# A hybrid layer's first block makes its output product by seven block products, and the sums are made elsewhere

## The chip, the cores and the metric

The kernel runs on one core of one Trainium2 chip. The time is that of the device, in microseconds (us): the median of the runs shown is compared. The engines are named as in the profile: PE (TensorE's matmuls) with PEld (its weight loads), DVE (VectorE), ACT (ScalarE), POOL (GpSimd) and SP (SyncE, which here only issues DMAs). POOL issues DMAs too.

## The reference

One layer is computed for a prompt of 2048 tokens and a sample of 64, each token a vector of 1024 numbers in 32-bit floats. All matrices below are 1024 x 1024 except the gate and projection of `p`.

```
h = rms_norm(x, g_pre)
vA, bA, cA, zA, q, f, iv, zB, gA, gB = split(h @ w_in)        # ten products
yA = (silu(zA) * bA * causal_conv3(cA * vA)) @ w_a_out        # path A
o  = hgrn2_scan(silu(q), 1 - fg, iv, log(fg)), normed         # path B, fg from f
yB = (o * silu(zB)) @ w_b_out
merged = sigmoid(gA) * yA + sigmoid(gB) * yB
out = merged @ w_o
x = x + rms_norm(out, g_post)                                 # first norm
gate = sigmoid(rms_norm(x, g_ple) @ w_ple_gate)               # second norm
x = x + (p @ w_ple_proj) * gate
```

## The kernel before

**Blocks.** The 2112 tokens are handled in three blocks of 768, 704 and 640 (`SIZES`, line 35). Everything lies with features on the 128 partitions and tokens along the row, so a 1024 x n activation is eight tiles of 128 x n. Each block has two token halves of 384, 352 or 320; that is the width of its matmuls.

**Matmuls in three parts.** A number is split into a high half, which the 32-bit matmul format takes as it is, and a low half, the rest (`split`, line 220: ACT casts, DVE subtracts). A product is hi x hi + hi x lo + lo x hi: three matmuls, which is why they come on lines 412 to 414, 559 to 561 and 594 to 596 in threes. The weights are split too. A low half that is used again is stored in DRAM ("low") and loaded later on SP's queue (line 269) instead of being computed again; `used_later` (line 245) decides which are stored.

**Seven products.** Most weight products are made by the seven products of Strassen's method in Winograd's form: a pair of column tiles and the two halves of the depth make a 2 x 2 matrix of blocks A11, A12, A21, A22, the activations likewise B11 to B22, and with sums S1 to S4 of the A's and T1 to T4 of the B's seven products replace eight. One product here is 4 k x 3 = 12 matmuls. `sgroup` (line 397) makes all seven for one pair of tiles, one after another; it makes the gates and most of `w_in`. `in_turn` (line 527) makes the first of the seven for all four pairs, then the second for all four, and so on; its operands (`operand_of`) are split just ahead of their product. In the middle and the last block W_A (`w_a_out`), W_B (`w_b_out`) and W_O (`w_o`) go this way. In the first block they go by plain products: `gemms` (line 637) and `gemm` load 8 x 2 weight tiles of 128 x 512 and make 384 matmuls for each matrix.

**The sums of the weights.** S1 to S4 and their low halves have to be in DRAM before `in_turn` can use them. `prepare_sums` (line 359) makes them in four groups for each matrix. A group loads four weight tiles, forms four sums on DVE (lines 387 to 393), stores each (line 376), splits it and stores its low half (line 379); all its DMAs are on POOL's queue. In the first block it makes those of W_A and W_B, in steps put into the loops of `merge`, with three buffers named "s" for the low halves (`shared`); low halves that `in_turn` and `sgroup` load use the same three buffers for three of every seven (`low_tile`). In the middle block it makes those of W_O in path A, with ring tiles instead.

**The end of a block.** `merge` (or `merge_in_turn`) makes yA, yB and the merged tiles; then W_O (`final_out`, or `out_in_turn`); then, while PE works on the next block's first seven gate groups (`run(fills, LEAD)`, 7 x 7 = 49 products), the steps of `final_norm` (line 1281) are put between the products; then `final_gate`. `operands` (line 755) makes the next block's T1 to T4 during W_O. The norm's steps: squares of W_O's result (`sum_squares`, ACT squares and DVE adds on line 707), column sums over the partitions by PE (`col_rstd`, line 685) and a power on POOL, a spread of the factors by PE (line 669), eight tiles scaled and added to x with their squares summed, the column sums and spread of the second norm, eight tiles split for `final_gate`.

**What sets the order.** A scheduler orders each engine's instructions by program order, marked priorities and its own estimate of times, and the order is then fixed. Weight loads and casts are marked urgent. `spread_out` (line 1349) puts a plan into `hooks`: one entry after each product, a number that says how many steps of the norm run there. `placed()` keeps a step's matmuls from going ahead of the product that they are put behind, and `behind_all` does that on the other engines. The plan for the norm was, in the middle block,

```
(1, 1, 1, 1, 0, 1, 0, 1) + (0, 1) * 8 + (0, 0, 1, 0, 1) + (0, 1) * 8
```

that is: four steps of squares, column sums at hook 5, spread at 7, eight norm steps, the second norm's column sums at hook 26 and spread at 28, eight splits up to hook 44. In the first block it was `(0, 1, 0, 1) + (0, 1, 0) * 8 + (0, 0, 1, 0, 1) + (0, 1) * 8`, with the squares made during W_O.

Of the kernel before, what the change touches and what calls it, by code (L numbers as in the profile page):

```python
# [93 lines left out]
def hybrid_step(  # L94
# [31 lines left out]
    def nm(s):  # L126
        uid[0] += 1
        return f"{s}_{uid[0]}"
# [113 lines left out]
    def sum_tile(dt=F32):  # L242
        return wp.tile([P, 4, P], dt, tag="s", name=nm("s"), bufs=3)

    def used_later(idx, part):

        if GA * 8 <= idx < GB * 8 + KB - 2:
            return part in ("S1", "S2", "S3", "S4")  # L250
        if idx in (GB * 8 + KB - 1, QQ * 8):
            return part != 0
        if W_A <= idx < W_G:
            lower = (idx - W_A) % KB >= KH
            return not lower if idx >= W_O and part == 0 else lower if idx < W_O and part == 1 else idx >= W_O
        return True

    def split_w(raw, key=None, spread=False):
# [100 lines left out]
    def prepare_sums(firsts, shared):  # L359


        groups = [(idx + g, idx + KH + g) for idx in firsts for g in range(KH)]

        def tile_of(dt=F32):
            return rt(4 * P, dt).rearrange("p (k c) -> p k c", c=P)

        def load(i1, i2):
            out = [tile_of() for _ in range(4)]
            for t, (i, h) in zip(out, ((i1, 0), (i2, 0), (i2, 1), (i1, 1))):
                G.dma_start(t, w_blk[i, h])  # L370
            return out

        def keep(name, i1, s):
            sums.setdefault(i1, {})[name] = dram.tile([P, 4, P], F32, tag=f"{name}_{i1}", name=nm(name), bufs=1)
            lows[i1, name] = dram.tile([P, 4, P], F32, tag=f"lo{name}_{i1}", name=nm("low"), bufs=1)
            G.dma_start(sums[i1][name], s)
            lo = sum_tile(F32R) if shared else tile_of(F32R)
            split(s, lo, lo)
            G.dma_start(lows[i1, name], lo.bitcast(F32))

        nxt = load(*groups[0])
        yield
        for n, (i1, _) in enumerate(groups):
            a11, a21, a22, a12 = nxt
            if n + 1 < len(groups):
                nxt = load(*groups[n + 1])
            V.tensor_tensor(a22, a21, a22, ALU.add)
            keep("S1", i1, a22)
            V.tensor_tensor(a21, a11, a21, ALU.subtract)
            keep("S3", i1, a21)  # L390
            V.tensor_tensor(a11, a22, a11, ALU.subtract)
            keep("S2", i1, a11)
            V.tensor_tensor(a12, a12, a11, ALU.subtract)
            keep("S4", i1, a12)
            yield
# [238 lines left out]
                hook()  # L634
        return pss

    def gemms(idx0, act, segs, by_k=False, late=KB - 1):

        j0, j1 = 0, KB
        if len(segs) > 1:  # L640
            yield from gemm_late([idx0, idx0 + 1], act, segs, late)
            j0 = 2
        if by_k:
            j1 -= 2
        for j in range(j0, j1):
            yield gemm(idx0 + j, act, segs)
        if by_k:
            yield from gemm_by_k([idx0 + j for j in range(j1, KB)], act, segs)


    def tiles_of(n):
# [103 lines left out]
    def operands(hc, rs, load, early=False):  # L755


        pair = None
        for i in range(KH):
            pair = pair or [load(k) for k in (i, i + KH)]  # L760
            for k, xk in zip((i, i + KH), pair):
                scaled_x(xk, k, rs)
            hc["B11"].append(narrow(half(pair[0], 0)))
            yield
            sums_of(hc, pair)
            yield
            hi, lo = split_rt(pair[1])
            hc["B21"].append((half(hi, 0), half(lo, 0)))
            hc["B22"].append((half(hi, 1), half(lo, 1)))
            pair = [load(k) for k in (i + 1, i + 1 + KH)] if early and i + 1 < KH else None  # L770
            yield

    ends, summed = [], []
# [404 lines left out]
            paced(dma)  # L1178
        return t

    def merge(bl, a, kept, extra):

        segs = bl["segs"]
        ob, m, mg, loaded = [], [], [], {}

        def fetch(kind, j):
            if j < KB:
                loaded[kind, j] = reload(kept[kind, j])

        fetch(GA, 0)  # L1190
        fetch("o", 0)
        for j, pss in enumerate(gemms(W_A, a, segs)):
            fetch(GA, j + 1)
            fetch("o", j + 1)
            if j == KB - 1:
                fetch(GB, 0)
            sg = loaded.pop((GA, j))
            for s, ps in zip(segs, pss):
                V.tensor_tensor(sg[:, cols_of(s)], ps, sg[:, cols_of(s)], ALU.mult)
            m.append(sg)  # L1200
            ob.append(split_rt(loaded.pop(("o", j))))
            if j in (2, 4, 6):
                next(extra, None)
        for j, pss in enumerate(gemms(W_B, ob, segs)):
            fetch(GB, j + 1)
            sg = loaded.pop((GB, j))
            for s, ps in zip(segs, pss):
                V.tensor_tensor(sg[:, cols_of(s)], ps, sg[:, cols_of(s)], ALU.mult)
            V.tensor_tensor(sg, sg, m[j], ALU.add)  # L1209
            mg.append(split_rt(sg))  # L1210
            if j in (0, 2, 4, 6, 7):
                next(extra, None)
        return mg

    def merge_in_turn(a, kept, mg):

# [28 lines left out]
            dict(idx=W_B, order=IN_TURN, raw=ob, sink=sink_b, anew=("A11", "A12")),  # L1245
        ], loads

    def final_out(segs, mg, xo, acc):

        for j, pss in enumerate(gemms(W_O, mg, segs, True)):  # L1250
            xo.append(rt())
            for s, ps in zip(segs, pss):
                A.copy(xo[j][:, cols_of(s)], ps)
            if j < KB - 2:
                sum_squares(j, xo[j], acc, width[0])
            yield
        for j in range(KB - 2, KB):
            sum_squares(j, xo[j], acc, width[0])
        yield

    def out_in_turn(mg, xo, acc, last):


# [14 lines left out]
        stage["sink"] = sink  # L1278
        return stage

    def final_norm(bl, segs, xo, acc, h2, kept, squares=False):


        c = slice(segs[0]["off"], segs[-1]["off"] + hn())
# [189 lines left out]
    for bi, bl in enumerate(blocks):  # L1474
# [26 lines left out]
        if first:  # L1501
            next(sums_ahead)
        mg, xo, h2, acc = [], [], [], rt()
        if first:
            mg = merge(bl, a, kept, sums_ahead)
        else:
            stages, loads = merge_in_turn(a, kept, mg)
            stages.append(out_in_turn(mg, xo, acc, bl["last"]))
            loads(W_A, -1)
            for idx, n in in_turn(stages, a_first):  # L1510
                loads(idx, n)
                if nxt and (idx, n) == (W_B, 6):
                    hc = new_operands()
                    with sized_to(nxt):
                        ops = sized(nxt, operands(hc, spread_all(cols), partial(load_x, nxt), True))
                    spread_out((ops, (0, 1, 0, 1, 0, 1, 0) * KH))
                elif nxt:
                    pass
                elif (idx, n) == (W_B, 5):
                    ph = [split_rt(raw) for raw in load_p(bl, G)]  # L1520
                elif (idx, n) == (W_O, 4):
                    norms = [final_norm(bl, [s], xo, acc, h2, None) for s in segs]
                    spread_out((norms[0], (1, 0, 1, 1, 1, 0, 1, 0)))
            if nxt:
                xo.extend(stages[-1]["mid"])
        if nxt:
            if first:
                hc = new_operands()
                with sized_to(nxt):
# [67 lines left out]
```

## Time and profile before

| | |
|---|---|
| median of 3 runs | 2611.29 us (2609.13 to 2613.52) |
| profiled execution | 2615.63 us, span 2613.6 us |
| granted PE clock, mean | 0.998 |
| PE, DVE, ACT, POOL busy | 99%, 65%, 56%, 14% |
| DMA | 717.92 MB, mean 275 GB/s |
| first block: W_A, W_B, W_O | from 700.7, about 768 and 836.8 us |
| next block's leading gate groups | 904.1 to about 1008 us |
| middle block: W_A, W_B, W_O, gate groups | from about 1590, 1644, 1698 and 1755 us |

A row of a group reads: line, engine, operation, output <- input with shape, count, busy us and mean ns of one. A row of waits reads: who waited for whom, us in total, times, longest. A row of the timeline has start and duration in us, and in brackets the time that its engine was idle before it and what ended that. PEq, SPq and POOLq are the engines' queues. Times of instructions overlap in PE's pipeline, so the pace is read from their starts. The tile names of this program: `pg` and `pa` are PSUM tiles, `raw`, `hi` and `lo` weights and their halves, `s` the three shared buffers, `S` and `low` the sums and low halves in DRAM, `r` the 48 ring tiles, `hf` half tiles.

### The profile page before, as it was taken

What the parts mean: (1) busy time and instruction counts of PE and PEld (TensorE: products, weight loads), DVE (VectorE), ACT (ScalarE), POOL (GpSimd) and SP (SyncE); (2) the same over time, 40 slices, a digit from 0 to 9 for tenths busy, and PEclk for the clock granted to TensorE, in tenths of its full rate; (3) what the DMA queues carried; (4) which work ended last, traced back from release to release, by engine and by line L of the source; (5) the groups of instructions that cost most, each with busy time, mean ns of one, the idle gap of its engine ahead of it and who ended that gap; (6) DMA issues with size and microseconds to landing.
All of it is one profiled execution on the core that took longest, in us unless ns stands there. A gap on an engine that the chain in (4) does not pass through costs nothing. (4 is left out here: it accounts for less than half of the span.)

```text
span 2613.6 us, 47303 instructions
## 1 busy us (share of the span) xinstructions
PE 2588.3 (99%) x16532; PEld 2575.7 (99%) x16532; DVE 1710.0 (65%) x3417; ACT 1472.4 (56%) x2852; POOL 352.9 (14%) x653
## 2 busy tenths in 40 slices
PE   8999999999999999999999999999999999999999
PEld 8999999999999999999999999999999999999998
DVE  7887788788757665465564456887435555336867
ACT  6655565554433564466564555566456665446675
POOL 2000000110143121111111221102100001001111
PEclk9999999999999999999999999999999999999999
DMA  8677667788788598866768998988887877999985
GB/s 322 219 243 243 230 224 245 268 300 269 266 330 281 197 324 266 284 222 205 266 225 284 354 383 310 323 276 310 294 278 246 268 249 261 299 299 312 339 269 202
DMA packets 350686, 717.92 MB, mean 275 GB/s; under 512 B 42960, under 2 KB 47600, under 8 KB 350448
## 3 DMA queue, kind: packets, MB, share of 16 engines
q1 hardware_dynamic: 312624, 566.17, 64.3%
q0 software_dynamic: 37536, 148.68, 15.7%
q8 instruction: 130, 2.13, 0.3%
q14 instruction: 108, 0.88, 0.1%
q10 hardware_dynamic: 288, 0.05, 0.0%
HBM read 521.52 MB, written 193.22 MB: 273 GB/s over the span
## 5 line engine op out<-in xcount | busy, mean ns | idle before, releaser
L412 PE MATMUL pg<-r,hi 128*128 128x320 f32 (+2 forms) x3304 | 1084.7, 328 | 0.7 <-ACT hi L220 0.7
L413 PE MATMUL pg<-r,hi 128*128 128x320 f32 (+2 forms) x3304 | 1068.4, 323 | 0.0
L414 PE MATMUL pg<-r,lo 128*128 128x384 f32 (+2 forms) x2356 | 768.3, 326 | 4.2 <-DMA lo<-low 4.2
L268 ACT CAST hi<-raw 128x512 fp32r<-128x512 f32 x678 | 417.7, 620 | 485.5 <-PE pg L413 176.2
L412 PEld LDWEIGHTS pg<-r,hi 128*128 128x128 f32 x3304 | 622.1, 188 | 1.6 <-ACT hi L220 1.0
L413 PEld LDWEIGHTS pg<-r,hi 128*128 128x128 f32 x3304 | 622.4, 188 | 0.0
L414 PEld LDWEIGHTS pg<-r,lo 128*128 128x128 f32 x2356 | 442.7, 188 | 5.6 <-DMA lo<-low 5.6
L414 PE MATMUL pg<-r,s 128*128 128x352 f32 (+1 forms) x948 | 300.5, 317 | 1.7 <-DMA s<-low 1.7
L220 ACT CAST hi<-raw 128x512 fp32r<-128x512 f32 x276 | 168.8, 621 | 199.9 <-PE pg L595 66.0
L595 PE MATMUL pg<-r,hi 128*128 128x384 f32 (+2 forms) x768 | 253.4, 330 | 0.0
L594 PE MATMUL pg<-r,hi 128*128 128x384 f32 (+2 forms) x768 | 253.0, 330 | 0.2 <-ACT hi L268 0.2
L220 DVE TENSOR_TENSOR lo<-raw,hi 128x512 fp32r<-128x512 f32 x248 | 169.6, 688 | 102.7 <-ACT hi L220 99.8
L596 PE MATMUL pg<-r,lo 128*128 128x384 f32 (+2 forms) x688 | 228.1, 332 | 0.0
L560 PE MATMUL pg<-r,hi 128*128 128x352 f32 (+1 forms) x656 | 207.0, 317 | 0.0
L559 PE MATMUL pg<-r,hi 128*128 128x352 f32 (+1 forms) x656 | 204.5, 318 | 0.0
L220 DVE TENSOR_TENSOR r<-r,r 128x320 fp32r<-128x320 f32 (+7 forms) x282 | 172.9, 632 | 43.9 <-ACT r L220 43.1
L220 ACT CAST hi<-s 128x512 fp32r<-128x512 f32 x160 | 99.2, 620 | 173.0 <-PE pg L413 161.5
L414 PEld LDWEIGHTS pg<-r,s 128*128 128x128 f32 x948 | 178.8, 189 | 2.5 <-DMA s<-low 2.5
L220 ACT CAST r<-r 128x320 fp32r<-128x320 f32 (+7 forms) x282 | 153.1, 574 | 40.8 <-DVE r L1209 11.9
L426 ACT COPY hf<-pg 128x352 f32<-128x352 f32 (+2 forms) x354 | 156.7, 445 | 5.4 <-PE pg L414 5.2
L220 DVE TENSOR_TENSOR lo<-s,hi 128x512 fp32r<-128x512 f32 x160 | 110.3, 690 | 63.5 <-ACT hi L220 58.7
L594 PEld LDWEIGHTS pg<-r,hi 128*128 128x128 f32 x768 | 144.0, 188 | 0.4 <-ACT hi L268 0.4
(394 smaller groups left out, 4113.3 us busy)
## 6 DMA issues: line engine op xcount, KB each, us to landing
raw<-w_blk SPq DMA_DIRECT2D x586, 256.0 KB, 3.9
raw<-S SPq DMA_DIRECT2D x408, 256.0 KB, 4.1
lo<-low SPq DMA_DIRECT2D x398, 256.0 KB, 3.9
low<-lo SPq DMA_DIRECT2D x287, 256.0 KB, 3.2
s<-low SPq DMA_DIRECT2D x280, 256.0 KB, 3.9
S<-s SPq DMA_DIRECT2D x152, 256.0 KB, 2.9
r<-w_blk POOLq DMA_DIRECT2D x48, 256.0 KB, 6.7
S<-r POOLq DMA_DIRECT2D x48, 256.0 KB, 6.3
```

The costliest lines, as they stand in the source:

```text
L220: return A.copy(hi, src).ins, V.tensor_tensor(lo, src, hi.bitcast(F32), ALU.subtract).ins
L268: A.copy(hi, raw)
L412: add(hi[:, k, :], xhi, start=start and k == 0, stop=False)
L413: add(hi[:, k, :], xlo, start=False, stop=False)
L414: last[0] = add(lo[:, k, :], xhi, start=False, stop=k == KH - 1).ins
L426: copied = A.copy(got[n], ps[bank])
L559: add(hi[:, k, :], xhi, start=start and k == 0, stop=False)
L560: add(hi[:, k, :], xlo, start=False, stop=False)
L594: T.matmul(ps, hi[:, k % 4, :], xhi[:, c], start=k == ks[0], stop=False)
L595: T.matmul(ps, hi[:, k % 4, :], xlo[:, c], start=False, stop=False)
L596: last[0] = T.matmul(ps, lo[:, k % 4, :], xhi[:, c], start=False, stop=k == ks[-1]).ins
```

## The change

The first block's W_O goes through `in_turn` with `out_in_turn`, like the middle block's; `final_out` goes away and `gemms` loses its options. `merge` becomes a generator, leaves the merged tiles unsplit, and makes the first operands of W_O after its seventh W_B tile; at that point the next block's first x tiles and spread factors are asked for as well (`next_ops`). `prepare_sums` makes W_O's and W_A's sums in the first block and W_B's in the middle block. For W_O it also makes and stores the low halves of A11, A12 and A22 (`keep_low`), which the plain products stored before. `final_norm` makes the squares itself in the first block too, both blocks use one plan, and in it the second norm's column sums stand at hook 28 and the last split at hook 46.

```diff
@@ used_later
-        if W_A <= idx < W_G:
-            lower = (idx - W_A) % KB >= KH
-            return not lower if idx >= W_O and part == 0 else lower if idx < W_O and part == 1 else idx >= W_O
+        if W_A <= idx < W_O:
+            return part == 1 and (idx - W_A) % KB >= KH
@@ prepare_sums
+        def keep_low(key, s):
+            lows[key] = dram.tile([P, 4, P], F32, tag=f"lo{key}", name=nm("low"), bufs=1)
+            lo = sum_tile(F32R) if shared else tile_of(F32R)
+            split(s, lo, lo)
+            G.dma_start(lows[key], lo.bitcast(F32))
...
-        for n, (i1, _) in enumerate(groups):
+        for n, (i1, i2) in enumerate(groups):
             a11, a21, a22, a12 = nxt
             if n + 1 < len(groups):
                 nxt = load(*groups[n + 1])
+            if i1 >= W_O:
+                for key, s in (((i1, 0), a11), ((i1, 1), a12), ((i2, 1), a22)):
+                    keep_low(key, s)
@@ operands
+        pair = [load(k) for k in (0, KH)]
+        yield
         for i in range(KH):
-            pair = pair or [load(k) for k in (i, i + KH)]
...
-            pair = [load(k) for k in (i + 1, i + 1 + KH)] if early and i + 1 < KH else None
+            pair = [load(k) for k in (i + 1, i + 1 + KH)] if i + 1 < KH else None
@@ merge
-            mg.append(split_rt(sg))
+            mg.append(sg)
             if j in (0, 2, 4, 6, 7):
                 next(extra, None)
-        return mg
+            yield
@@ final_norm
-        if squares:
+        if kept is not None:
             for j in range(KB):
                 sum_squares(j, xo[j], acc, width[0])
@@ the loop over blocks
-        sums_ahead = prepare_sums((W_A, W_B), True) if first else prepare_sums((W_O,), False) if bi == 1 else iter(())
+        sums_ahead = prepare_sums((W_O, W_A), True) if first else prepare_sums((W_B,), False) if bi == 1 else iter(())
...
+        def next_ops():
+            with sized_to(nxt):
+                made = sized(nxt, operands(hc, spread_all(cols), partial(load_x, nxt)))
+                next(made)
+            return made
...
+        stages = [out_in_turn(mg, xo, acc, bl["last"])]
         if first:
-            mg = merge(bl, a, kept, sums_ahead)
+            for j, _ in enumerate(merge(bl, a, kept, mg, sums_ahead)):
+                if j == KB - 2:
+                    a_first.extend(narrow(half(t, 0)) for t in mg[:KH])
+                    ops = next_ops()
+            spread_out((ops, (0, 1, 0, 1, 0, 1, 0) * KH))
+            loads = lambda idx, n: None
...
-            if first:
-                hc = new_operands()
-                with sized_to(nxt):
-                    ops = sized(nxt, operands(hc, spread_all(cols), partial(load_x, nxt)))
-                for j, _ in enumerate(final_out(segs, mg, xo, acc)):
-                    if j in (1, 3, 5, 7):
-                        run(ops, 3)
-            norm = sized(bl, final_norm(bl, segs, xo, acc, h2, kept, not first))
-            start = (0, 1, 0, 1) + (0, 1, 0) * KB if first else (1, 1, 1, 1, 0, 1, 0, 1) + (0, 1) * KB
-            spread_out((norm, start + (0, 0, 1, 0, 1) + (0, 1) * KB))
+            norm = sized(bl, final_norm(bl, segs, xo, acc, h2, kept))
+            spread_out((norm, (1, 1, 1, 1, 0, 1, 0, 1) + (0, 1) * KB + (0, 0, 0, 0, 1, 0, 1) + (0, 1) * KB))
```

More of the change, by code (lines that the diff above doesn't have):

```diff
@@ L635, in gemm_by_k, with gemms @@
         return pss
[L637 to L645, printed above, removed]
+    def gemms(idx0, act, segs):
+        yield from gemm_late([idx0, idx0 + 1], act, segs, KB - 1)
+        for j in range(2, KB):
             yield gemm(idx0 + j, act, segs)
-        if by_k:
-            yield from gemm_by_k([idx0 + j for j in range(j1, KB)], act, segs)
     def tiles_of(n):
@@ L1246, in merge_in_turn @@
         ], loads
[L1248 to L1259, printed above, removed]
     def out_in_turn(mg, xo, acc, last):
@@ L1509, in hybrid_step @@
+        if first:
+            for j, _ in enumerate(merge(bl, a, kept, mg, sums_ahead)):
[4 more added lines that the diff above has]
+            loads = lambda idx, n: None
+        else:
+            before, loads = merge_in_turn(a, kept, mg)
+            stages = before + stages
             loads(W_A, -1)
-            for idx, n in in_turn(stages, a_first):
-                loads(idx, n)
-                if nxt and (idx, n) == (W_B, 6):
-                    hc = new_operands()
-                    with sized_to(nxt):
[L1515 to L1523, printed above, removed]
```

34 lines of the change are left out of this document (19 added, 15 removed).

## The prediction

> **What bounds the kernel now.** I read the page's busy times first, then what PE waited for, then windows over the stages that the change touches.
>
> ```profile
> PE 2588.3 (99%) x16532; PEld 2575.7 (99%) x16532; DVE 1710.0 (65%) x3417; ACT 1472.4 (56%) x2852; POOL 352.9 (14%) x653
> ```
>
> ```profile
> PE pa L1153 <- ACT r L220: 6.9, 1, 6.9
> PE pg L414 <- DMA lo<-low: 4.2, 5, 1.6
> PE pa L685 <- DVE r L707: 3.3, 2, 2.7
> ```
>
> PE is busy for 99% of the span. Its largest wait (6.9 us) is at the very start, where the change does not reach. So the time moves only if PE gets less to do, gets new gaps, or loses old ones; work on other engines counts only where it makes a gap. In the windows, the columns are length, then busy us and instructions of PE, PEld, DVE, ACT, POOL, then granted clock, DMA share and GB/s. The rows are the first block's W_A, its W_O, its seven leading gate groups, and the middle block's W_O.
>
> ```profile
> 700.70:768.00 67.30, 67.30 (x385) 67.30 (x384) 48.72 (x76) 26.59 (x42) 31.80 (x60) 1.00 0.91 339
> ```
>
> ```profile
> 836.80:904.10 67.30, 67.30 (x387) 67.30 (x386) 44.29 (x65) 31.36 (x55) 9.69 (x18) 1.00 0.65 215
> 904.10:998.00 93.90, 91.04 (x575) 89.91 (x575) 63.28 (x95) 59.37 (x108) 17.54 (x30) 1.00 0.85 297
> ```
>
> ```profile
> 1698.00:1752.00 54.00, 53.52 (x327) 51.77 (x326) 47.00 (x94) 38.18 (x82) 4.28 (x8) 1.00 0.86 287
> ```
>
> The first block's W_O has PE full at clock 1.00 with DMA only 65% busy. The middle block already does its W_O by seven products, so its row shows what the first block will look like.
>
> **Part 1: PE's work in the first block's W_O.** Its edges on PE's timeline:
>
> ```profile
> 836.79 0.42 PE L594 MATMUL pg<-r,hi 128*128 128x384 f32 x1
> ```
>
> ```profile
> 903.92 0.34 PE L596 MATMUL pg<-r,lo 128*128 128x384 f32 x1
> 904.10 0.32 PE L412 MATMUL pg<-r,hi 128*128 128x352 f32 x1
> ```
>
> By the code that is 8 column tiles x 2 token halves x 8 k x 3 = 384 matmuls from 836.79 to 904.10: 67.31 us, 0.1753 us each (durations overlap, so the step counts and not the 0.34). Seven products are 7 x 4 x 4 x 3 = 336, of the same width. 48 go: 48 x 0.1753 = **-8.4 us**, all on the path, since PE never paused here.
>
> **Part 2: what feeds those products.** Out go 16 weight loads, 16 casts, 16 subtractions, 12 stores of low halves on SP's queue, and the eight splits of the merged tiles. In come, on SP's queue, 28 loads of weights or sums and 28 of low halves, 56 x 256 KB = 14.7 MB in 58.9 us, 249 GB/s; 28 casts; 28 operand splits with their sums. The middle block does the same instruction list on 352 columns: DVE 47.0 of 54 us, DMA 0.86. Scaled by 384/352, DVE needs at most 51 of 58.9 us. PE paid this there:
>
> ```profile
> 1727.54 0.75 PE L559 MATMUL pa<-r,hi 128*128 128x352 f32 x3 [0.22 <-ACT r L220]
> 1728.45 0.43 PE L560 MATMUL pa<-r,hi 128*128 128x352 f32 x1 [0.16 <-DVE r L220]
> ```
>
> I take the same 0.38: **+0.4**. Where the two blocks differ is DMA that is left over at the start. The sums come in eight groups on POOL's queue, paced by the merge loop, and the last begins inside W_O:
>
> ```profile
> 841.85 0.69 DVE L387 TENSOR_TENSOR r<-r,r 128x512 f32<-128x512 f32 x1 [4.08 <-DMA r<-w_blk]
> ```
>
> ```profile
> r<-w_blk POOLq DMA_DIRECT2D x48, 256.0 KB, 6.7
> S<-r POOLq DMA_DIRECT2D x48, 256.0 KB, 6.3
> low<-s POOLq DMA_DIRECT2D x32, 256.0 KB, 5.6
> ```
>
> ```profile
> r<-x_fm POOLq DMA_DIRECT2D x16, 352.0 KB, 7.0
> ```
>
> A group is 4 loads, 4 sums, 4 low halves: 3.1 MB. It now meets a stage that itself asks for 249 GB/s, plus the next block's x. Bounds: 0, if the prefetched weights cover it, to 3 us (3.1 MB over about 14 us is 220 GB/s; with 249 and x some 500 against the 406 quoted below, so a quarter of 14 us). I take 1, nearer zero, since by the code four casts and seven low halves can lie ready: **+1.0**.
>
> **Part 3: sums and low halves.** W_O's four groups each write three more low halves: 12 casts, 12 subtractions and 12 issues on POOL, beside W_A and the start of W_B.
>
> ```profile
> L220 ACT CAST hi<-s 128x512 fp32r<-128x512 f32 x160 | 99.2, 620 | 173.0 <-PE pg L413 161.5
> ```
>
> ```profile
> L220 DVE TENSOR_TENSOR lo<-s,hi 128x512 fp32r<-128x512 f32 x160 | 110.3, 690 | 63.5 <-ACT hi L220 58.7
> ```
>
> ```profile
> ACT s L220 <- DMA low<-s: 16.9, 11, 4.0
> ```
>
> 12 x 0.62 = 7.4 us of ACT and 12 x 0.69 = 8.3 of DVE, in a window where DVE is busy 48.7 and ACT 26.6 of 67.3 us, and the merged tiles' splits leave the same loop: hidden, 0. The wait that is added: ACT waits for one of three "s" buffers until a low half is stored (so far 16.9 us over 32 of them, 4.0 at most). Queued behind it are the weight casts, and on POOL the fetches of the saved gates. At the same rate 12 more cost ACT 6 us of waiting, spread over four groups; PE showed no gap in W_A with the earlier 16.9. I take 0, with those 6 us as the upper end.
>
> W_B's sums move to the middle block's path A, where W_O's were, by the same instructions. They are wanted one stage (54 us) earlier; the last low half is issued there at 1565 (the row), and W_B begins near 1644:
>
> ```profile
> L379 POOL DMA_DIRECT2D low<-r x16: 542/542/547, 1481.3 to 1565.4; - x16
> ```
>
> Hidden, 0. So is the next block's first x pair, asked for two products earlier.
>
> **Part 4: the second norm, middle block.** Its column sums stand on PE's queue (L685), and PE stopped there for the last squares:
>
> ```profile
> 1811.19 0.89 DVE L707 TENSOR_TENSOR r<-r,r 128x704 f32<-128x704 f32 x1
> ```
>
> ```profile
> 1812.23 2.45 PE L685 MATMUL pa<-ones,r 128*128 128x1 f32 x12 [2.73 <-DVE r L707]
> ```
>
> ```profile
> 1814.96 0.47 PE L414 MATMUL pg<-r,lo 128*128 128x320 f32 x1
> 1815.23 0.47 PE L412 MATMUL pg<-r,hi 128*128 128x320 f32 x1
> ```
>
> ```profile
> 1820.91 0.31 PE L414 MATMUL pg<-r,lo 128*128 128x320 f32 x1
> 1821.06 0.31 PE L412 MATMUL pg<-r,hi 128*128 128x320 f32 x1
> ```
>
> ```profile
> 1809.40:1812.20 2.80, 0.10 (x1) 0.00 (x0) 2.74 (x6) 1.63 (x3) 0.54 (x1) 1.00 0.99 338
> 1812.20:1814.70 2.50, 2.47 (x13) 2.50 (x14) 0.85 (x3) 0.00 (x0) 0.88 (x1) 0.56 1.02 405
> 1814.70:1819.40 4.70, 4.70 (x19) 4.70 (x20) 0.65 (x2) 1.78 (x4) 1.99 (x3) 0.51 0.81 293
> ```
>
> The gap is 2.73 us, and behind it the granted clock is 0.56 and then 0.51 until 1819.4. There a matmul steps 0.27 instead of 0.15: 17 of them cost 2.0 more, and the 12 column sums 1.06 more than the undisturbed 1.39 below. The stall is worth 2.73 + 2.0 + 1.06 = 5.8 us. How far does it move? The plan lets the sums go after 27 products (hook 26); by the count below they stood after 111/4 = 27.75. After the change they may go after 29.
>
> ```profile
> 970.54 1.39 PE L685 MATMUL pa<-ones,r 128*128 128x1 f32 x12
> ```
>
> ```profile
> 1755.20:1809.40 54.20, 34.14 (x111) 20.73 (x111) 1.00 0.86 299
> ```
>
> So 1.25 products move ahead, 15 matmuls x 0.1465 = 2.2 us; 0.5 of the gap stays, too short to lower the clock (1.59 below did not). Gain 2.2 + 3.06 = **-5.2**. Bounds: 0, if the squares come as much later, to -5.8.
>
> **Part 5: the first block's gates.** Its final norm takes the middle block's rhythm: the eight squares leave W_O for four steps here, the eight norm steps come every second product instead of every third, and the second norm after 29 products instead of 31. Gaps, first and middle block:
>
> ```profile
> 911.59 0.43 PE L412 MATMUL pg<-r,hi 128*128 128x352 f32 x1 [0.75 <-ACT hi L220]
> 939.89 0.43 PE L414 MATMUL pg<-r,s 128*128 128x352 f32 x1 [0.52 <-DMA s<-low]
> 949.49 0.43 PE L414 MATMUL pg<-r,lo 128*128 128x352 f32 x1 [1.59 <-DMA lo<-low]
> ```
>
> ```profile
> 1757.96 0.41 PE L414 MATMUL pg<-r,s 128*128 128x320 f32 x1 [0.95 <-DMA s<-low]
> 1796.17 0.41 PE L414 MATMUL pg<-r,lo 128*128 128x320 f32 x1 [1.02 <-DMA lo<-low]
> ```
>
> ```profile
> 936.00:950.00 14.00, 11.89 (x72) 11.31 (x72) 9.20 (x14) 6.81 (x13) 2.15 (x4) 1.00 1.03 406
> ```
>
> The first block pays 2.9 us now, the middle one 2.0 besides its norm. In the new rhythm DMA is asked for more (x in and out within 3.9 instead of 5.8 us), against a ceiling seen at 406 GB/s. I take 2.0 + the 0.5 of part 4, less 2.9, so about 0, **+0**; bounds -2.9 (all gaps gone) and +5.8 (the whole norm stall appears here). The middle block's last splits come two products later too, at the 47th of 49; 3.5 us remain for a cast and a subtraction: 0.
>
> **Sum:** -8.4 + 0.4 + 1.0 - 5.2 + 0 = -12.2 us. The profiled execution took 2615.63 us (span 2613.6 and 2.0 around it), 4.3 above the median of 2611.29 and above the slowest shown, 2613.52. I take the same difference off both: 2603.4 profiled and **2599.1** in the median.
>
> **A rule weighed.** The row says that 2.73 us of idling halved the clock. [...]
>
> **The rivals.**
> A. The clock fell in the profiled execution only, or the norm's sums are as late as before: of 5.2 us only 2.2, or nothing, is there in the median. For it: the profile is 4.3 us slower than the median. Against: the order is fixed in the program. Time 2611.3 - 8.4 + 1.4 - 2.2 = 2602.1, or 2604.3 with no gain at all.
> B. The first block gets the norm stall that the middle one had, 5.8 us, with 3 us of waits at the start of W_O: 2599.1 + 5.8 + 2.0 = 2607. For it: the same rhythm, DMA at its ceiling. Against: 29 products instead of 27, and each product is 10% longer there.
> C. Slower: W_A's sums slide into W_O. Three "s" buffers serve both the sums' low halves and three of seven of the products' low loads; the latter have priority. W_O's 58.9 us carry 58.9 x 406 = 23.9 MB; its weights and x take 14.7 + 2.9, so it decides from two groups (6.3 MB) on. All four are 12.6 MB, 30.2 in all, 74 us instead of 59: +15 us, and where the waits come as five gaps like the 2.73, each costs 3.06 more: 2614 to 2629. Against: the groups are tied to the merge loop, and now only the last one begins 5 us into W_O.
> D. The waits for low halves in the gates (2.9 + 2.0) go as well: 2594.
>
> **How the numbers follow.** The forecast has 0.50, A 0.15, B 0.15, C 0.10, D 0.10. 0.2%, about what can be told from no change, is 5.2 us here: faster is below 2606.1, slower above 2616.5. The forecast, A, D and a little of B are faster: 0.77; the rest of B and the low end of C are the same: 0.14; C's upper part is slower: 0.09. The range goes from D's 2594 less a microsecond to past B: 2593 to 2611; the forecast alone has 2595 to 2604.
>
> **What would show it.** Right: 16484 matmuls on PE; L594 to L596 without the first block's W_O, and 128x384 matmuls on lines 559 to 561 for some 59 us; no gap at L685 in the middle block and no clock of 0.5 there. Wrong: a clock below 1.00 after the first block's W_O begins; waits for lo<-low or s<-low of more than 3 us within it; sums (L387) still being made well after its start; L685 waiting for L707 in the first block.

## The result, and the profile after

The change makes the kernel faster by a quarter of a percent: median 2604.98 us (2603.03 to 2611.69, 11 runs) against 2611.29 us (2607.77 to 2615.26, 11 runs); ratio 0.9976, 95% interval 0.9968 to 0.9984, so 4.2 to 8.4 us less. The forecast was 2599.1, 12.2 us less: the sign is right, and nearly half of the gain is missing. The profiled execution of the changed kernel took 2604.98 us, its span 2603.2.

The page of the changed kernel, busy times:

```profile
PE 2579.6 (99%) x16484; PEld 2566.8 (99%) x16484; DVE 1729.1 (66%) x3469; ACT 1487.7 (57%) x2896; POOL 358.5 (14%) x665
```

The 48 matmuls are gone. PE was busy 8.7 us less. What PE waited for in the changed kernel, behind the 6.9 us at the start, which are unchanged (us in total, times, longest; the lines have moved, L420 was L414, L600 was L594, L567 was L561, L684 was L685):

```profile
PE pg L420 <- DMA lo<-low: 3.8, 4, 1.8
PE pg L600 <- ACT hi L220: 2.4, 1, 2.4
```

Of the 3.3 us at the norm's column sums 0.2 are left. In their place stands a wait that the kernel before does not have: 2.4 us at L600 for a weight's high half, made by ACT. The timeline of the changed kernel has, in this order, that gap in the first block's W_B, the edges of W_O, and the second norm's sums in the middle block:

```profile
789.39 0.45 PE L600 MATMUL pg<-r,hi 128*128 128x384 f32 x1 [2.39 <-ACT hi L220]
...
841.15 0.34 PE L565 MATMUL pg<-r,hi 128*128 128x384 f32 x1
...
900.45 0.32 PE L418 MATMUL pg<-r,hi 128*128 128x352 f32 x1
...
1807.05 1.39 PE L684 MATMUL pa<-ones,r 128*128 128x1 f32 x12
```

The middle block's sums now have no gap and take 1.39 us, not 2.45. W_O lasts from 841.15 to 900.45, 59.30 us instead of 67.31. But it begins later. The same two stretches, W_A with W_B and then W_O, as windows of the kernel before (columns: length, busy us and instructions of PE, PEld, DVE, ACT, POOL, clock, DMA share, GB/s):

```profile
700.83:836.79 135.96, 135.96 (x781) 135.96 (x781) 92.94 (x145) 49.55 (x78) 55.94 (x104) 1.00 0.82 295
836.79:904.10 67.31, 67.31 (x387) 67.31 (x386) 44.30 (x65) 31.36 (x55) 9.69 (x18) 1.00 0.65 215
```

and of the changed one:

```profile
700.43:841.15 140.72, 138.15 (x781) 137.50 (x781) 106.27 (x171) 54.00 (x92) 68.45 (x128) 0.99 0.94 337
841.15:900.45 59.30, 59.30 (x337) 58.62 (x337) 51.50 (x92) 43.17 (x84) 4.26 (x8) 1.00 0.91 308
```

W_O gives 8.0 us, W_A and W_B take 4.8 of them back. The rest of this text calls the two stretches together the first block's stretch: 203.27 us before, 200.02 after.

Why ACT was late shows in its timeline in the changed kernel, ahead of the gap:

```profile
783.00 1.34 ACT L220 CAST s<-r 128x512 fp32r<-128x512 f32 x2 [2.41 <-DMA low<-s]
784.71 0.62 ACT L220 CAST s<-r 128x512 fp32r<-128x512 f32 x1 [0.36 <-DMA low<-s]
788.20 0.62 ACT L220 CAST s<-r 128x512 fp32r<-128x512 f32 x1 [2.87 <-DMA low<-s]
788.72 1.66 ACT L220 CAST hi<-raw 128x512 fp32r<-128x512 f32 x3
```

The casts of the low halves that are made ahead need one of three "s" buffers, and wait until an earlier low half is stored. The three casts of W_B's weights stand behind them in ACT's order. From 700 to 840 us, before and after:

```profile
ACT s L220 <- DMA low<-s: 16.4, 10, 4.0
```

```profile
ACT s L220 <- DMA low<-s: 59.7, 28, 6.6
```

The wait is 3.6 times as long (over the whole trace 59.7 us against 16.9), not 12/32 longer. The extra twelve are not all of it: the 32 casts of low halves in the kernel before began between 708.7 and 848.6 us, the last four of them inside W_O, and the 44 of the changed kernel between 706.8 and 830.4 us, all ahead of W_O. So more work on the sums lies in a shorter time.

### The profile page after: what moved, and what is told of

It is laid out like the page before. It is cut to its first block, busy times and chain, and to the rows that moved or that the text cites. A ratio compares the mean times of both kernels' runs of the same rounds, so it can differ in the third digit from the quotient of the medians.

```text
span 2603.2 us, 47398 instructions
## 1 busy us (share of the span) xinstructions
PE 2579.6 (99%) x16484; PEld 2566.8 (99%) x16484; DVE 1729.1 (66%) x3469; ACT 1487.7 (57%) x2896; POOL 358.5 (14%) x665
## 4 chain that ended last, share of the span: by engine, by line
PE 92%; DMA 4%; DVE 1%; issue 1%; ACT 1%; POOL 0%; SPq 0%; DVEq 0%; POOLq 0%; ACTq 0%
PE pg L418 20%; PE pg L420 19%; PE pg L419 19%; PE pg L565 4%; PE pg L566 4%; PE pg L567 4%; PE pg L600 3%; PE pg L602 3%; PE pg L601 3%; PE pa L1045 1%; PE pa L1081 1%; PE pa L1083 1%; DMA lo<-low 1%; PE pa L1031 1%; PE pa L1030 1%
## 5 line engine op out<-in xcount | busy, mean ns | idle before, releaser
L418 PE MATMUL pg<-r,hi 128*128 128x320 f32 (+2 forms) x3304 | 1085.6, 329 | 0.3 <-ACT r L809 0.3
L419 PE MATMUL pg<-r,hi 128*128 128x320 f32 (+2 forms) x3304 | 1068.3, 323 | 0.0
L420 PE MATMUL pg<-r,lo 128*128 128x384 f32 (+2 forms) x2356 | 768.3, 326 | 3.8 <-DMA lo<-low 3.8
L267 ACT CAST hi<-raw 128x512 fp32r<-128x512 f32 x706 | 435.0, 620 | 501.4 <-PE pg L419 169.5
L418 PEld LDWEIGHTS pg<-r,hi 128*128 128x128 f32 x3304 | 621.8, 188 | 1.0 <-ACT r L809 0.6
L419 PEld LDWEIGHTS pg<-r,hi 128*128 128x128 f32 x3304 | 622.1, 188 | 0.0
L420 PEld LDWEIGHTS pg<-r,lo 128*128 128x128 f32 x2356 | 442.8, 188 | 4.9 <-DMA lo<-low 4.9
L420 PE MATMUL pg<-r,s 128*128 128x352 f32 (+1 forms) x948 | 299.8, 316 | 1.5 <-DMA s<-low 1.5
L220 ACT CAST hi<-raw 128x512 fp32r<-128x512 f32 x260 | 158.8, 621 | 160.4 <-PE pg L419 47.8
L566 PE MATMUL pg<-r,hi 128*128 128x320 f32 (+2 forms) x752 | 239.1, 320 | 0.0
L565 PE MATMUL pg<-r,hi 128*128 128x320 f32 (+2 forms) x752 | 237.1, 320 | 0.0
L600 PE MATMUL pg<-r,hi 128*128 128x384 f32 (+2 forms) x640 | 211.0, 331 | 2.6 <-ACT hi L220 2.4
L601 PE MATMUL pg<-r,hi 128*128 128x384 f32 (+2 forms) x640 | 210.8, 330 | 0.0
L220 DVE TENSOR_TENSOR lo<-raw,hi 128x512 fp32r<-128x512 f32 x232 | 158.2, 686 | 72.9 <-ACT hi L220 70.7
L602 PE MATMUL pg<-r,lo 128*128 128x384 f32 (+2 forms) x560 | 185.6, 332 | 0.2 <-DVE lo L220 0.2
L420 PEld LDWEIGHTS pg<-r,s 128*128 128x128 f32 x948 | 178.3, 188 | 2.3 <-DMA s<-low 2.3
L567 PE MATMUL pg<-r,lo 128*128 128x320 f32 (+2 forms) x484 | 153.8, 319 | 2.1 <-DMA lo<-low 2.1
```

The costliest lines, as they stand in the source:

```text
L220: return A.copy(hi, src).ins, V.tensor_tensor(lo, src, hi.bitcast(F32), ALU.subtract).ins
L267: A.copy(hi, raw)
L418: add(hi[:, k, :], xhi, start=start and k == 0, stop=False)
L419: add(hi[:, k, :], xlo, start=False, stop=False)
L420: last[0] = add(lo[:, k, :], xhi, start=False, stop=k == KH - 1).ins
L565: add(hi[:, k, :], xhi, start=start and k == 0, stop=False)
```

## The experiments

In the diffs long lines are shortened. Two theories of the missing gain. **S:** three "s" buffers are too few, and ACT's order carries the wait to the weights. **M:** the DMA engines, 0.94 busy in W_A and W_B, are the bound, and the buffers only show it. A third reading, **J**, was that the gap belongs to that one execution, and that the gain is lost elsewhere, in later blocks. Before that, the two parts of the change are taken apart.

### The norm and the first block, each alone

The change without the middle block's later norm:

```diff
-  (1, 1, 1, 1, 0, 1, 0, 1) + (0, 1) * KB + (0, 0, 0, 0, 1, 0, 1) + ...
+  (1, 1, 1, 1, 0, 1, 0, 1) + (0, 1) * KB + ((0, 0, 0, 0, 1, 0, 1) if first else (0, 0, 1, 0, 1)) + ...
```

> The changed kernel, with the middle block's second norm back at its old place (two products earlier); the first block is left as changed. My theory (part 4 of the prediction): the stall of 2.73 us in front of the column sums of L684, and the half clock behind it, come back in every execution, 5.8 us together: 2604.98 + 5.8 = 2610.8 us. Rival A (the clock fell only in the profiled execution of before): a gap of some 2.7 us at most, clock 1.00 behind it, so 2605 to 2607.7 us.

The kernel before with only that norm moved:

```diff
-  start + (0, 0, 1, 0, 1) + (0, 1) * KB
+  start + ((0, 0, 1, 0, 1) if first else (0, 0, 0, 0, 1, 0, 1)) + (0, 1) * KB
```

> The kernel before, with only the middle block's second norm two products later. My theory: the whole stall goes, 5.8 us, and nothing else moves: 2611.29 - 5.8 = 2605.5 us. Rival A: only the gap is there in most executions, so 2608.5 us, or no gain, 2611.3. If this part alone gives nearly all of the 6.3 us that the change gave, then the first block's edit gave next to nothing net: its shorter W_O (8.0 us in the profiles) was given back in front of it.

Measured: the change without the norm 2610.94 us, ratio to the kernel before 0.9996 (0.9988 to 1.0004); the norm alone 2606.11 us, 0.9982 (0.9973 to 0.9990), beside 2611.47 for the kernel before. By the medians the norm's move is worth 5.4 us on the old kernel and 6.0 on the changed one, and the first block's whole edit 0.5 us without the new norm, 1.1 with it. The interval of the first block's edit alone, from 3.1 us faster to 1.0 slower, includes no gain at all and leaves out the forecast's 7.0. Nearly all of the gain is the norm's.

The stall came back in the first of the two, at nearly its old size. Timeline and windows (columns: length, PE, clock, DMA share, GB/s):

```profile
1807.03 2.25 PE L684 MATMUL pa<-ones,r 128*128 128x1 f32 x12 [2.38 <-DVE r L706]
```

```profile
1807.03:1809.30 2.27, 2.27 (x13) 0.61 1.05 416
1809.30:1812.00 2.70, 2.70 (x11) 0.50 0.71 274
```

The first block's stretch in this kernel, whose first block has the changed kernel's code, and in the one with the norm alone:

```profile
700.16:840.45 140.29, 136.86 (x782) 1.00 0.94 336
840.45:903.20 62.75, 59.53 (x337) 1.00 0.90 303
```

```profile
699.78:903.05 203.27, 203.27 (x1165) 1.00 0.77 268
```

203.04 us and 203.27 us: in this execution the shorter W_O gained nothing at all. W_B had gaps of 1.51 and 1.72 us, and W_O itself one of 3.21 for a low half that was loaded. So the first half of J falls: a loss in front of W_O is there again, with other gaps. Whether gain is lost in later blocks as well, this does not tell.

### The suspects taken away

The twelve extra low halves not made ahead, but by W_O's products as they come to them:

```diff
-            if i1 >= W_O:
-                for key, s in (((i1, 0), a11), ((i1, 1), a12), ((i2, 1), a22)):
-                    keep_low(key, s)
```

> The changed kernel, but the first block's twelve low halves of W_O's own quarters (A11, A12, A22) are not made ahead during W_A and W_B: W_O's products make them as they come to them, and store them then. 12 splits and 12 stores of 262 KB (3.1 MB) move out of W_A and W_B, and 12 loads of 3.1 MB go. Theory S and rival M both expect the stall at L600 in W_B to go: 2604.98 - 4.2 = 2600.8 us. If the stall stays, it is not the twelve extra low halves that brought it but the order of the sums or their own 32. A price can show in W_O: ScalarE and VectorE get 12 splits of 0.69 us there in 59.3 us; if the first products wait for them, up to 2 us come back (2602.8).

W_A's sums left out of the first block (the comment stands for the lines that have the middle block read W_O's sums in their place, at the same traffic):

```diff
-  prepare_sums((W_O, W_A), True) if first
+  prepare_sums((W_O,), True) if first      # sums and lows of W_A point to W_O's
```

> The changed kernel with W_A's sums left out of the first block: the middle block reads W_O's sums and low halves in their place, so its work and traffic are the same. In the first block 16 loads and 32 stores of 262 KB (12.6 MB) and the work on 16 sums go from W_B. Theory M (the first block's work on the sums, at 0.95 busy DMA engines, eats the gain of the shorter W_O): W_B and W_O run without stalls, and the 7.0 us that part 1 and 2 of the prediction expected are there: 2606.11 (only the norm moved) - 7.0 = 2599.1 us, at least 4.2 us below 2604.98. Rival J (the stall in the profiled W_B is a matter of that execution, the gain goes elsewhere, in later blocks): 2603 to 2605 us.

W_B's sums left out of the middle block's path A (the last block then reads W_O's):

```diff
-  prepare_sums((W_B,), False) if bi == 1 else iter(())
+  iter(())                                 # sums and lows of W_B point to W_O's
```

> The changed kernel with W_B's sums left out of the middle block's path A: the last block reads W_O's sums and low halves in their place. 16 loads and 32 stores of 262 KB go from a stretch in which the DMA engines are full (1460 to 1540 us). By part 3 of the prediction these sums cost nothing there, as W_O's cost nothing there before: 2604 to 2606 us. Rival J (part of the missing gain is lost from the middle block on): 2602 us or less.

The 16 low halves of W_A's sums left to the middle block:

```diff
-            keep_low((i1, name), s)
+            if not W_A <= i1 < W_B:
+                keep_low((i1, name), s)
```

> The changed kernel, but the 16 low halves of W_A's sums are not made ahead in the first block; the middle block's W_A makes and stores them where it takes the sums. In W_B 16 of the 44 low halves and 4.2 MB of stores go; W_A of the middle block loses 16 loads of 4.2 MB and gets 16 splits and 16 stores. Theories S and M: W_B without its stall, -4.2 us, W_A of the middle block free, as no_extra showed for W_O: 2600.8 us. If the middle block's W_A then waits for VectorE's low halves, up to 2 us come back.

The stretch without the twelve extra low halves, without W_A's sums, and without W_B's sums:

```profile
703.05:841.44 138.39, 137.31 (x781) 1.00 0.91 329
841.44:900.90 59.46, 59.45 (x338) 1.00 0.87 279
```

```profile
701.37:837.42 136.05, 136.05 (x781) 1.00 0.75 265
837.42:896.69 59.27, 59.27 (x338) 1.00 0.89 295
```

```profile
701.38:841.01 139.63, 136.86 (x782) 1.00 0.93 336
841.01:902.75 61.74, 59.55 (x338) 1.00 0.90 310
```

Without W_A's sums W_A and W_B have no gap and the stretch is 195.32 us, 7.95 under 203.27: this is nearly the 8.4 that part 1 promised, so in the profiled execution it is the work on the sums that eats it. Without the extra low halves it is 197.85. The kernel without W_B's sums has the changed first block: 201.37 us there. ACT's waits for a store of a low half, from 700 to 840 us, were 37.0 us without the extra low halves, which leaves the same 32 as before, and 29.9 without W_A's sums.

The times say less. Without the extra low halves 2604.13 us, 0.9974 (0.9965 to 0.9983); without W_A's sums 2603.74, 0.9964 (0.9951 to 0.9978); without W_B's 2603.25, 0.9965 (0.9953 to 0.9978); with W_A's low halves made later 2604.65, 0.9971 (0.9960 to 0.9981), and a gap of 3.73 us in W_B all the same. That gap has another cause: it came at 808.17 us, after the last store of a low half had been given out there (785.7 us), and VectorE had idled 5.36 us for a quarter that a sum needed, with the subtraction for a weight's low half behind it. All four intervals overlap that of the change (0.9968 to 0.9984). Those that were expected at 2600.8 or 2599.1 missed, and 2603.74 lies in the 2603 to 2605 that J forecast. The profiled execution without W_A's sums was the slowest of its five. Its stretch was 4.7 us shorter than the changed kernel's, but the rest of its span was 6.9 us longer. It had gaps in code that had not been touched, 2.91 us at 1241, 1.79 at 1749 and 1.93 at 2449; behind the first the granted clock was 0.54 for 3.73 us. Why the medians did not gain is open. Without W_B's sums the time lies between the two forecasts, so whether these sums cost some 1 to 2 us in path A is not settled.

### More buffers

All low halves of the sums in ring tiles:

```diff
-            lo = sum_tile(F32R) if shared else tile_of(F32R)
+            lo = tile_of(F32R)
```

> The changed kernel, with the low halves of the sums made ahead in the first block held in tiles of the large ring instead of the three s buffers. Theory S (ScalarE waits in its order for an s buffer until a low half is stored, and the casts of W_B's weights stand behind it): ScalarE's waits for low<-s fall from 59.7 us to under 10 in W_A and W_B, the gap of 2.39 us at L600 and the lower clock behind it go, 2604.98 - 4.2 = 2600.8 us. Rival M (the DMA engines, 0.95 busy in W_B, are the bound, and the buffers only show it): ScalarE or TensorE waits as long for something else (raw, or a ring tile), and the time stays at 2604 to 2606 us.

A fourth "s" buffer for one tile of the ring, and for one "lo" buffer:

```diff
-RING = 48
+RING = 47
-    tag="s", name=nm("s"), bufs=3
+    tag="s", name=nm("s"), bufs=4
```

```diff
-    tag="s", name=nm("s"), bufs=3
+    tag="s", name=nm("s"), bufs=4
-    tag="lo", name=nm("lo")
+    tag="lo", name=nm("lo"), bufs=3
```

> The changed kernel with four s buffers instead of three, paid for with one of the 48 tiles of the large ring. Theory S (three s buffers are the limit: ScalarE waits for one in its order): ScalarE's waits for low<-s fall by half or more, the stall at L600 in W_B shrinks from 4.2 us to under 1, time 2601 to 2602 us. Theory M (the stores cannot drain faster, the DMA engines are 0.95 busy): a fourth buffer is full as soon as the third, the waits stay within a quarter of 59.7 us and the time at 2604 to 2606 us. One ring tile less may cost something in other stages; waits for r on other lines would show it.

> The changed kernel with a fourth s buffer again, now paid for with one of the four lo buffers, so the ring keeps its 48 tiles. With the ring at 47 the four buffers left W_A and W_B without a gap (140.00 of 140 us busy between 700 and 840 us), and the time was lost in other stages. Theory S: the same here, W_B without a gap and 2604.98 - 4.2 = 2600.8 us, if lo can do with three. Against it: W_G, W_A and W_B take every low half of a weight from lo, and a third instead of a fourth buffer may stall TensorE there for lo; then more than 2605 us.

Every fourth low half in a ring tile:

```diff
-            lo = sum_tile(F32R) if shared else tile_of(F32R)
+            lo = sum_tile(F32R) if shared and len(lows) % 4 else tile_of(F32R)
```

> The changed kernel with every fourth low half made ahead in the first block in a tile of the ring, the others in the three s buffers (all of them in the ring cost 8 us: TensorE waited 5.4 us for operands of W_O, whose tiles come from the same ring). Theory S: one low half in four off the three buffers does what a fourth buffer does, W_B without a gap over 1 us, 2601 us. Theory that the ring is as scarce as the buffers: waits at L565 to L567 for r of over 1 us in W_O, 2604 us or more.

The stretch with the fourth buffer, first with 47 ring tiles, then with three "lo" buffers:

```profile
699.88:835.98 136.10, 136.10 (x781) 1.00 0.96 355
835.98:895.25 59.27, 59.27 (x338) 1.00 0.89 298
```

```profile
700.65:838.35 137.70, 136.59 (x781) 1.00 0.96 357
838.35:897.61 59.26, 59.26 (x338) 1.00 0.88 290
```

195.37 and 196.96 us: the fourth buffer brings back 7.9 and 6.3 of part 1's 8.4 us, with all the sums and low halves made. The DMA engines moved more in that time, 355 and 357 GB/s against 337. So the DMA engines were not at their limit in the changed kernel, and M falls for its W_A and W_B. S stands as to the gap, with two different payments, but not as to the wait: it was to fall by half or more, and with 47 ring tiles it fell by less than a quarter, which M had forecast; with three "lo" buffers it was 37.9 us.

```profile
ACT s L220 <- DMA low<-s: 45.9, 24, 6.8
```

The total of ACT's waits does not tell whether PE stops: there was no gap in W_A and W_B with 45.9 or 29.9 us of it, and gaps of 2.11 and 2.39 with 36.1 and 59.7. What counts is whether a weight's cast that PE needs soon stands behind one of them.

The times went the other way: 2615.25 us with 47 ring tiles, 1.0015 (1.0005 to 1.0024), and 2630.63 with three "lo" buffers, 1.0071 (1.0059 to 1.0084). What was taken is missed elsewhere. With the ring at 47, ScalarE waits some 32 us for output tiles to be stored in the middle block's final gate, with casts of weights behind these waits, and TensorE idles 7.6 us between 1890 and 1930, where the changed kernel has no gap; with three "lo" buffers TensorE waits for loaded low halves all through the sevens:

```profile
PE pg L420 <- DMA lo<-low: 17.2, 12, 3.6
PE pg L567 <- DMA lo<-low: 8.1, 9, 3.1
```

With all low halves in the ring, ScalarE's wait for "s" stores in W_A and W_B was gone, and the time was 2612.95 us, 1.0005 (0.9996 to 1.0014). S had forecast W_B without its gap, but there was one of 3.82 us: VectorE waited 8.57 us for a quarter that a sum needed, and the subtraction for a weight's low half stood behind it. Then W_O waited for its operands. That the ring was now short of tiles is likely, but not shown.

```profile
789.19 0.69 DVE L393 TENSOR_TENSOR r<-r,r 128x512 f32<-128x512 f32 x1 [8.57 <-DMA r<-w_blk]
```

```profile
790.54 0.69 PE L602 MATMUL pg<-r,lo 128*128 128x384 f32 x1 [3.82 <-DVE lo L220]
```

```profile
856.30 0.69 PE L566 MATMUL pg<-r,hi 128*128 128x384 f32 x1 [4.42 <-DVE r L220]
```

With one low half in four in the ring the median is 2599.52 us, 0.9957 (0.9946 to 0.9968): 8.4 to 14.1 us faster than the kernel before, and with an interval that only touches the change's. It is the fastest of all, but the two intervals do not settle that it beats the change. Its profile does not show where it gains. That execution took 2603.85 us, the second slowest of six, and its stretch was hardly better than the change's, 199.55 us against 200.02, with the gap at the old place, where S had forecast none over 1 us; ScalarE's wait for the stores was down from 59.7 to 36.1 us:

```profile
789.14 0.44 PE L600 MATMUL pg<-r,hi 128*128 128x384 f32 x1 [2.11 <-ACT hi L220]
```

```profile
ACT s L220 <- DMA low<-s: 36.1, 18, 8.4
```

That its faster executions lack the gap is possible after the runs with four buffers, but it is not shown.

### GpSimd's order

In the changed kernel GpSimd gives out the loads of the next group ahead of stores that hold the buffers:

```profile
785.17 0.54 POOL L1175 DMA_DIRECT2D r<-g__1217_4995  x1
785.71 2.12 POOL L370 DMA_DIRECT2D r<-w_blk  x4
787.82 0.54 POOL L381 DMA_DIRECT2D S<-r  x1
788.35 0.54 POOL L377 DMA_DIRECT2D low<-s  x1
```

So the loads were put behind the stores, alone and with one low half in four in the ring:

```diff
-            if n + 1 < len(groups):
-                nxt = load(*groups[n + 1])
             ...
             keep("S4", i1, a12)
+            if n + 1 < len(groups):
+                nxt = load(*groups[n + 1])
             yield
```

> The changed kernel, but each group of sums asks for the next group's four quarters after its own stores, not ahead of them. In the trace of the changed kernel GpSimd gives out two reloads and these four loads (785.17 to 787.83 us) ahead of the stores of two low halves that were done before; the s buffers stay taken, and ScalarE's next cast, with W_B's weights behind it, came at 788.20. Theory Q (part of the wait for s is GpSimd's order): the stall of 2.39 us at L600 falls under 1 us, 2601 to 2602 us. Rival: the buffers are taken by the transfers themselves, the stall stays, 2604 to 2606 us; or the later loads reach the sums late (VectorE waits for r<-w_blk), more than 2606 us.

> The changed kernel with both edits: every fourth low half in a ring tile (alone 2599.52 us) and the next group's loads after the stores. If the two help the same wait, the sum is not reached: theory S expects 2598 to 2600 us, theory S with Q some 2 us below the one alone, 2597.5 us. If the later loads cost, 2601 us or more.

Both missed: 2614.02 us, 1.0007 (0.9998 to 1.0016), and 2617.68, 1.0019 (1.0010 to 1.0028). With the loads late, alone, the stores were indeed waited for less, 20.3 us, but the casts now waited for the sums, and these for their quarters (ScalarE's and VectorE's waits, 700 to 840 us):

```profile
ACT s L220 <- DVE r L391: 28.8, 5, 8.7
ACT s L220 <- DMA low<-s: 20.3, 11, 3.6
ACT s L220 <- DMA r<-w_blk: 16.8, 4, 7.0
```

```profile
DVE r L391 <- DMA r<-w_blk: 14.0, 4, 4.9
```

TensorE's gap at the same place became 6.61 us, and W_O got one of 4.27. This theory fell. With the gaps of 3.73 and 3.82 us above it widens S, though: a store, a sum or a loaded quarter may be what is late, and on ScalarE or VectorE the halves of the weights stand behind it.

## Why the prediction was half right

**Part 1 (-8.4) was right.** 16484 matmuls; W_O took 59.30 us instead of 67.31, and 59.3 to 59.5 in the other kernels whose stretch is shown and whose W_O had no gap.

**Part 2 (+1.4) varied from one profiled execution to the next.** In the changed kernel's, W_O had no gap, so +0.4 (59.30 against 336 x 0.1753 = 58.9). In two other kernels with the same first block it had one gap for a low half loaded from DRAM, 3.21 and 2.19 us, which ended some 5 us after its start; with them W_O was 3.85 and 2.84 us longer than 58.9, against bounds of 0.4 to 3.4. The +1.0 stood for a last group of sums inside W_O. There was none: the last store of a low half was given out at 832.23, before W_O began, so rival C did not come either, and these gaps have another cause, which is open.

**Part 3 (0) is the step that failed.** It put twelve more low halves beside W_A and W_B at nothing because DVE and ACT had time left, and scaled ACT's wait for the buffers in proportion, by 6 us at most. The wait grew by 43 us, and W_A with W_B became 4.8 us longer than before, 4.3 and 3.7 in the two other kernels with the same first block. These lie under the upper end of 6 us, but that end was reckoned from an added wait a seventh as long. Over the whole stretch, parts 2 and 3 together ate 5.15 us of 8.4 in the changed kernel (203.27 to 200.02), 8.2 in the one with the old norm and 6.5 in the one without W_B's sums. With a mean of 6.6 where the forecast had 1.4, the first block's edit is worth some 1.8 us in the stretch, against 0.5 and 1.1 in the medians and 7.0 in the forecast. What the sum left out is that a wait for a buffer is not a sum of durations, and that the groups themselves would come closer together, in 124 us instead of 140. A group of W_O's now asks for seven low halves at once, a buffer comes free only when its store is done, and behind the cast that waits stand those of the weights that PE needs next. How much of it each of these makes was not measured. The working even named the casts as standing behind the wait, and then priced it by PE having shown no gap so far.

**Part 4 (-5.2) was right.** 5.4 and 6.0 us by the medians; the gap went whole, so the 0.5 us that was to remain did not. Rival A (at most 2.2 us of gain in the median) is refuted: put back, the stall cost 6.0 us in the median of twelve runs, and the norm's move alone gave 2.6 to 7.1 us by its interval.

**Part 5 (0) came out a little better.** In the profiled execution the first block's gates had gaps of 1.57 us instead of 2.9, and no stall at the second norm, so rival B did not come. D did not either: waits for low halves stayed.

**The level.** I took the same 4.3 us off both profiles to come to medians. The changed kernel's profile lay on its median (2604.98 both), that of the kernel before 4.3 above. So 10.6 of the 12.2 us seemed to be there in the profiled executions, and 6.3 in the medians. The executions of one kernel differ by 4 to 10 us, and the profiles, one for each kernel, have gaps that come and go in stages that no edit touched. One profile of each does not settle a sum to 2 us.

## What to carry to other kernels

Work put beside a full engine is not free because the engines under it have time left: here W_A and W_B became 4.8 us longer, though DVE had been busy 92.94 and ACT 49.55 of 135.96 us. Look at what waits in the order of the engine that feeds the full one. When more items go through a fixed number of buffers, cost the wait by how many come at once and how long each is held; here 44 items instead of 32, in a shorter time, waited 3.5 times as long. When buffers are moved from one use to another, the loss appears in the stage that used them, so a stage's gain is believed only when the whole time has it: the fourth "s" buffer, paid for with a ring tile, gained 4.65 us on the changed kernel's stretch, and the median became 2615.25 us instead of 2604.98.

## What the runs showed of the hardware

In these profiles a gap's length did not tell whether the clock fell after it. At the same place in W_B the changed kernel idled 2.39 us and the kernel without W_B's sums 2.21 us. Windows from the end of each gap (length, PE, granted clock, DMA share, GB/s), first the changed kernel:

```profile
789.39:793.00 3.61, 3.43 (x11) 0.63 1.02 356
```

```profile
790.16 0.45 PE L600 MATMUL pg<-r,hi 128*128 128x384 f32 x1 [2.21 <-ACT hi L220]
```

```profile
790.16:794.00 3.84, 3.65 (x19) 1.00 0.95 375
```

11 matmuls in 3.6 us against 19 in 3.8. A gap of 1.83 us was followed by half clock in the changed kernel, and one of 3.21 us in the kernel with the old norm was not:

```profile
1253.43 0.43 PE L420 MATMUL pg<-r,lo 128*128 128x352 f32 x1 [1.83 <-DMA lo<-low]
```

```profile
1254.57:1257.98 3.41, 3.41 (x17) 0.50 1.04 409
```

```profile
846.27 0.44 PE L567 MATMUL pg<-r,lo 128*128 128x384 f32 x1 [3.21 <-DMA lo<-low]
```

```profile
846.27:850.00 3.73, 3.73 (x21) 1.00 1.03 369
```

Part 4's remark that gaps up to 1.59 us are too short to lower the clock holds for the 1.59 us that it quotes (the clock was 1.00 in the 10.5 us behind it), but is no bound. In the kernel without the extra low halves two shorter gaps came close together, and from 905.03 to 907.96 us a matmul then stepped 0.29 us, where before and after it was 0.16:

```profile
902.92 0.43 PE L417 MATMUL pg<-r,lo 128*128 128x352 f32 x1 [1.05 <-DMA lo<-low]
```

```profile
904.27 0.43 PE L417 MATMUL pg<-r,s 128*128 128x352 f32 x1 [0.59 <-DMA s<-low]
```

What makes the difference between these cases is not shown. How long the clock stayed low can be read for three gaps: 3.41 us for the one of 1.83 (the row above) and for the one of 2.39 in the changed kernel, and 6.82 us for part 4's 2.73 in the kernel before, each with 1.00 in the 3.4 us behind it. The changed kernel's first and the kernel before:

```profile
790.36:793.77 3.41, 3.41 (x12) 0.50 0.98 371
793.77:797.19 3.42, 3.42 (x21) 1.00 1.03 407
```

```profile
1812.55:1819.37 6.82, 6.82 (x29) 0.50 0.88 329
1819.37:1822.80 3.43, 3.43 (x28) 1.00 0.72 266
```

At a clock of 0.50 that is, by estimate, half of the time lost on top of the gap itself: 1.7 us for each of the first two and 3.4 for the third, for which part 4 counted 3.06 from the steps of the matmuls.
